# Inverting the recurrence's 32x32 blocks whole on VectorE, instead of joining 16x16 inverses by matmuls

## The chip, the cores and the metric

The kernel runs on one NeuronCore of a Trainium2 chip. The metric is the device time of one execution in microseconds (us). A core has five engines that each work through a queue of their own in order: TensorE (PE; its weight loads are shown as PEld), VectorE (DVE), ScalarE (ACT), GpSimd (POOL) and SyncE (SP), which here only starts DMAs. Results of matmuls go to PSUM, everything else lies in SBUF, and larger intermediates in device memory (HBM).

## What is computed

The reference is two transformer blocks on 1024 tokens of width 1024. The first block has gated linear attention, windowed attention and a feed-forward part. The second has an even layer (retention and an RWKV-7 recurrence, in both directions, over 1024 tokens and 256 tokens of context) and an odd layer (long convolutions and neighbourhood attention). The change concerns the RWKV-7 recurrence alone. Per head it is

```python
def rwkv7_scan(r, w, k, v, kk, a, s0):
    def step(s, inp):
        r_t, w_t, k_t, v_t, kk_t, a_t = inp
        sa = jnp.einsum('bhvk,bhk->bhv', s, -kk_t)
        s = s * w_t[:, :, None, :] + sa[..., None] * (kk_t * a_t)[:, :, None, :] + v_t[..., None] * k_t[:, :, None, :]
        return s, jnp.einsum('bhvk,bhk->bhv', s, r_t)
    ...
```

The kernel does it in chunks of 64 tokens. Within a chunk the terms `sa` of all tokens solve a triangular system: a unit lower triangular 64x64 matrix per head and chunk has to be inverted. Its two diagonal 32x32 blocks are inverted first, then joined by the off-diagonal block.

## The kernel before

All five engines' code is written as one Python program; a list scheduler of the framework decides, before the run, in which order each engine's instructions stand. It prefers what is written earlier in the program, as soon as it holds it to be ready, and fills the gaps with what is written later. That order is then fixed: an engine that waits for one instruction holds up all that stand behind it. In `mixers` the recurrence (`rwkv`) is written first and the retention projections (`ret_proj`) after it, so in the queue of TensorE projection matmuls (L217 to L219) fill the gaps of the recurrence. When they are used up, `ret_state` follows (matmuls L1370, and a chain on GpSimd), and the next stage begins when both it and the recurrence are done.

The recurrence has two directions of ten 128-token tiles. A batch is one tile of each direction, 64 blocks of 32x32 in all (2 directions, 2 chunks, 8 heads, 2 diagonal blocks). There are ten batches, and each goes through four parts:

- **Preparation** (`prep2`): decays, products and the four score matrices per chunk by matmuls (L1604, L1613, L1649, L1655); VectorE masks them out of PSUM (`wam`, L1657). The triangular blocks are written to HBM (`wlt`, L1661).
- **Inversion** (`invert`): L is loaded from HBM with one block half per partition, 128 partitions for 64 blocks of two diagonal 16x16 halves. VectorE then does a substitution column by column: a product with the known columns (`wtm`, L1681), then a reduction (L1682), 15 of each. The 16x16 inverses are written to HBM (`wrd`, L1684).
- **Merge** (`merge`, once per direction): the 16x16 inverses (`wdc`, L1696) and the 16x16 off-diagonal parts (`wnr`, L1697) are loaded; ScalarE spreads them into masked tiles (L1701, L1702), VectorE transposes (`wD`, L1703), and TensorE joins two 16x16 inverses to a 32x32 one with three groups of matmuls (L1709, L1712, L1721), with copies by ScalarE between and behind them (L1717, L1726). VectorE transposes the result (`wY`, L1731). Then the two 32x32 inverses are joined to the 64x64 one `wX` by two groups of matmuls (L1738, L1745) with ScalarE's copies (L1741, L1749).
- **Steps** (`chain`): two chunks per direction, four steps a batch. A step is five groups of matmuls (L1790, L1797, L1811, L1823, L1828). Between them stand copies by ScalarE and VectorE (`wrs`, L1793 and L1794; `wxv`, L1803 and L1805) and the state's update on VectorE (`wt`, L1816; `wxv`, L1782) and GpSimd (`wS`, L1783).

The order in the program is

```python
        prep(0)
        invert(0)
        prep(1)
        for bi in range(10):
            for s, (d, m) in enumerate(batches[bi]):
                merge(d, m, bi, s, bi)
            for s, (d, m) in enumerate(batches[bi]):
                chain(d, m, bi == 9)
            if bi < 9:
                invert(bi + 1)
            if bi < 8:
                prep(bi + 2)
```

so the inversion of the next batch has the steps of this one to hide behind, on the same VectorE. The tiles L, T and the products' tile have one buffer each. A step and a merge each take a two-bank PSUM tile (`p2`), of which there are two; a merge takes two in turn, one for the 16x16 joining and one for the rest.

Of the kernel before, what the change touches and what calls it, by code (L numbers as in the profile page):

```python
# [10 lines left out]
F32 = mybir.dt.float32  # L11
# [5 lines left out]
OP = mybir.AluOpType  # L17
AX = mybir.AxisListType
# [21 lines left out]
class Ker:  # L40
# [1507 lines left out]
    def rwkv(self, p):  # L1548
# [21 lines left out]
        T = p.tile([P, 16, 16], F32, name="wT")  # L1570

        hm = p.tile([P, 4], F32, name="whm")
        nc.sync.dma_start(hm, a["c_rwh"])

        N_ = p.tile([P, 8, 64], F32, name="wN")
        G_ = p.tile([P, 8, 64], F32, name="wG")
        for t in (N_, G_):
            nc.gpsimd.memset(t, 0.0)
# [4 lines left out]
        rt_d = [dr.tile([64, 2, 16, 16], F32, name=f"wrd{b}") for b in range(10)]  # L1583
# [3 lines left out]

        def by_rows(t, s, e, step, width, at):

            v = t[32 * s + 16 * e:32 * s + 16 * e + 16]  # L1590
            return bass.AP(tensor=v.tensor, offset=v.offset + at, ap=[[step, 64], [64 * step, 8], [1, width]])
# [76 lines left out]
        def invert(bi):  # L1668


            L = p.tile([P, 16, 16], F32, name="wL", tag="wL", bufs=1)
            for h in range(2):
                q = slice(16 * h, 16 * h + 16)
                nc.sync.dma_start(L[64 * h:64 * h + 64], lt_d[bi][:, q, q])
            nc.gpsimd.memset(T, 0.0)
            nc.gpsimd.memset(bass.AP(tensor=T.tensor, offset=T.offset, ap=[list(T.ap[0]), [17, 16]]), 1.0)
            tmp = p.tile([P, 256], F32, name="wtm", tag="wtm", bufs=1)
            for i in range(14, -1, -1):
                n = 15 - i
                tv = tmp[:, :n * n].rearrange("p (c j) -> p c j", j=n)  # L1680
                nc.vector.tensor_mul(tv, T[:, i + 1:, i + 1:], L[:, i:i + 1, i + 1:].to_broadcast([P, n, n]))  # L1681
                nc.vector.tensor_reduce(T[:, i + 1:, i], tv, axis=AX.X, op=OP.add, negate=True)  # L1682
            for h in range(2):
                nc.sync.dma_start(rt_d[bi][:, h], T[64 * h:64 * h + 64])  # L1684

        def merge(d, m, bi, s, xi):
# [3 lines left out]
            Y = p.tile([P, 2, 4, 32], F32, name="wY", tag="wY", bufs=1)  # L1690

            dc = p.tile([P, 8, 16], F32, name="wdc", tag="wdc", bufs=1)
            nr = p.tile([P, 8, 16], F32, name="wnr", tag="wnr", bufs=1)
# [990 lines left out]
```

## Time and profile before

| | us |
|---|---|
| median of 3 runs | 4260.48 (4253.2 to 4278.48) |
| profiled execution | 4259.86 |
| its span | 4258.1 |
| TensorE busy | 3871.4 (91%), 24649 instructions |
| TensorE weight loads busy | 3126.2 (73%) |
| VectorE busy | 1956.1 (46%), 2944 instructions |
| ScalarE busy | 1402.2 (33%), 2881 instructions |
| GpSimd busy | 1116.5 (26%), 1135 instructions |

Shares of the whole span are means over stages that have different limits. The recurrence runs from about 2123 to 2993 us. The views of the trace that are used below are: windows (busy time of each engine in a stretch, then the granted TensorE clock, the DMA share and GB/s), waits (who waited for whom, inferred from semaphores), groups of instructions by line, and the timeline (instructions in order of time, with what ended the idle time before them in brackets). In the windows the columns are PE, PEld, DVE, ACT and POOL where all engines are shown, and PE and PEld alone for a line of TensorE. In a group the columns are: line, engine, operation, output <- inputs, shapes, count, busy us, mean ns of one, and the idle time before them with its releasers. Where one row shows "+4 forms", its mean is over several shapes. Matmuls are pipelined and their ends are modelled, so a busy TensorE is not one at its peak.

### The profile page before, as it was taken

How to read it: one execution, taken by the hardware profiler on the slowest of the kernel's cores; microseconds unless marked ns; L12 is line 12 of the kernel's file. 1: busy time of each engine (PE TensorE's matmuls, PEld its weight loads, DVE VectorE, ACT ScalarE, POOL GpSimd, SP SyncE). 2: the span in 40 equal slices, each digit the busy share in tenths (PEclk: the TensorE clock that was granted, in tenths of full speed). 3: DMA queues.
4: the chain of work that ended last, by engine and by line, in shares of the span. 5: the costliest groups of instructions: out<-in, count | busy, mean ns of one | idle time of the engine just before them, and what ended most of it. 6: DMA issues, size and time to landing. Idle time of an engine off the chain costs nothing. (4 is left out here: it accounts for less than half of the span.)

```text
span 4258.1 us, 62069 instructions
## 1 busy us (share of the span) xinstructions
PE 3871.4 (91%) x24649; PEld 3126.2 (73%) x24649; DVE 1956.1 (46%) x2944; ACT 1402.2 (33%) x2881; POOL 1116.5 (26%) x1135
## 2 busy tenths in 40 slices
PE   7999989988999999699879898988789999998987
PEld 5788867776878888577777787777467777676776
DVE  4233433456443443633234444442556426653576
ACT  4333332215212222532244353443223324442211
POOL 1110202123111111201364233226530200003574
PEclk9999979998999999788898899986899999998998
DMA  5322237562141413332576555553764644324465
GB/s 200 122 97 77 89 105 257 207 242 102 57 151 60 139 63 101 138 140 102 184 218 172 165 139 147 165 151 106 229 200 144 235 134 119 104 77 152 153 199 202
DMA packets 474209, 621.96 MB, mean 146 GB/s; under 512 B 163201, under 2 KB 324403, under 8 KB 467776
## 3 DMA queue, kind: packets, MB, share of 16 engines
q1 hardware_dynamic: 423440, 416.26, 30.2%
q0 software_dynamic: 50480, 201.75, 14.4%
q8 instruction: 194, 3.18, 0.3%
q14 instruction: 95, 0.78, 0.1%
HBM read 423.34 MB, written 193.88 MB: 145 GB/s over the span
## 5 line engine op out<-in xcount | busy, mean ns | idle before, releaser
L217 PE MATMUL p<-hhi,whi 128*128 128x512 f32 x1056 | 417.1, 396 | 5.9 <-DVE hf L389 5.8
L218 PE MATMUL p<-hlo,whi 128*128 128x512 f32 x1056 | 415.7, 394 | 4.3 <-DVE hlo L391 4.3
L219 PE MATMUL p<-hhi,wlo 128*128 128x512 f32 x1056 | 415.0, 393 | 0.0
L217 PE MATMUL pf<-whi,hhi 128*128 128x512 f32 (+1 forms) x992 | 358.8, 363 | 19.1 <-ACT rqr L1279 10.3
L218 PE MATMUL pf<-wlo,hhi 128*128 128x512 f32 (+1 forms) x992 | 353.8, 357 | 7.7 <-POOL wlo L177 4.3
L219 PE MATMUL pf<-whi,hlo 128*128 128x512 f32 (+1 forms) x992 | 352.1, 356 | 0.0
L176 ACT CAST whi<-wraw 128x2048 fp32r<-128x2048 f32 (+1 forms) x123 | 193.1, 1574 | 457.1 <-PE pt L219 174.8
L177 DVE TENSOR_TENSOR wlo<-wraw,whi 128x2048 fp32r<-128x2048 f32 (+1 forms) x103 | 213.4, 2073 | 271.5 <-ACT whi L176 265.5
L217 PE MATMUL pf<-hhi,whi 128*128 128x512 f32 (+1 forms) x640 | 254.1, 397 | 4.4 <-ACT hyo L2047 1.5
L219 PE MATMUL pf<-hhi,wlo 128*128 128x512 f32 (+1 forms) x640 | 250.2, 391 | 2.5 <-DMA wlo<-wkl 2.5
L218 PE MATMUL pf<-hlo,whi 128*128 128x512 f32 (+1 forms) x640 | 250.0, 391 | 0.0
L217 PEld LDWEIGHTS pf<-whi,hhi 128*128 128x128 f32 x992 | 199.7, 202 | 58.7 <-ACT rqr L1279 11.2
L217 PE MATMUL pj<-whi,hhi 128*128 128x512 f32 (+1 forms) x560 | 216.7, 389 | 27.3 <-ACT whi L176 12.1
L217 PEld LDWEIGHTS p<-hhi,whi 128*128 128x128 f32 x1056 | 201.3, 191 | 54.3 <-DVE hf L389 6.2
L218 PEld LDWEIGHTS p<-hlo,whi 128*128 128x128 f32 x1056 | 201.0, 190 | 46.7 <-DVE hlo L391 5.3
L219 PEld LDWEIGHTS p<-hhi,wlo 128*128 128x128 f32 x1056 | 200.9, 190 | 43.1 <-issue 0.8
L218 PEld LDWEIGHTS pf<-wlo,hhi 128*128 128x128 f32 x992 | 200.0, 202 | 35.3 <-issue 6.6
L219 PE MATMUL pj<-whi,hlo 128*128 128x512 f32 (+1 forms) x560 | 214.2, 384 | 3.5 <-DVE hlo L381 3.5
L219 PEld LDWEIGHTS pf<-whi,hlo 128*128 128x128 f32 x992 | 198.9, 201 | 23.7 <-issue 2.6
L218 PE MATMUL pj<-wlo,hhi 128*128 128x512 f32 (+1 forms) x560 | 214.7, 384 | 0.3 <-DVE wlo L177 0.3
L217 PEld LDWEIGHTS pf<-hhi,whi 128*128 128x128 f32 x640 | 123.2, 193 | 36.1 <-issue 7.4
L217 PEld LDWEIGHTS pj<-whi,hhi 128*128 128x128 f32 x560 | 108.4, 194 | 54.6 <-ACT whi L176 12.3
(762 smaller groups left out, 8591.2 us busy)
## 6 DMA issues: line engine op xcount, KB each, us to landing
wraw<-w_in POOLq DMA_DIRECT2D x25, 1024.0 KB, 6.0
wraw<-w_ada POOLq DMA_DIRECT2D x24, 1024.0 KB, 7.8
wraw<-w_up POOLq DMA_DIRECT2D x22, 1024.0 KB, 6.1
whi<-wkh POOLq DMA_DIRECT2D x40, 512.0 KB, 5.4
wlo<-wkl POOLq DMA_DIRECT2D x40, 512.0 KB, 5.4
wraw<-ada_w POOLq DMA_DIRECT2D x32, 512.0 KB, 4.7
ox<-x SPq DMA_DIRECT2D x48, 256.0 KB
xp<-xl SPq DMA_DIRECT2D x48, 256.0 KB
```

What stands on the lines that cost most here:

```text
L176: nc.scalar.copy(hi[:, :n], raw[:, :n])
L177: self.we.tensor_sub(lo[:, :n], raw[:, :n], hi[:, :n].bitcast(F32))
L217: mm(out, L[0], R[0], start=first, stop=False)
L218: mm(out, L[0], R[1], start=False, stop=False)
L219: mm(out, L[1], R[0], start=False, stop=last)
```

## The change

The 32x32 blocks are inverted whole. L is loaded with all 32 rows of a block on a partition, as one contiguous 4 KB piece; each block stands on two partitions, and the one takes the even rows of the inverse, the other the odd rows (16 each). GpSimd writes -1 on L's diagonal and 1 on the inverse's, so that one formula holds for all rows. The substitution has 31 columns, each a product and a reduction. The inverse is written to HBM in rows of 128 bytes (`rt_d`), and a merge loads it with a row per partition (`wV`): that is the operand that `wY` was, and four transposes on VectorE per merge make the diagonal blocks of `wX` from it. All of the 16x16 joining goes: the loads of `wdc` and `wnr`, the masked tiles, the transpose `wD`, three groups of matmuls, and ScalarE's copies. A merge needs one `p2` tile instead of two. Line numbers shift: L1681 and L1682 become L1670 and L1671, `wX`'s transposes are L1687, L1738 and L1745 become L1694 and L1701, and the steps' matmuls L1746, L1753, L1767, L1779 and L1784.

```diff
-        T = p.tile([P, 16, 16], F32, name="wT")
+        T = p.tile([P, 16, 32], F32, name="wT")
...
-        rt_d = [dr.tile([64, 2, 16, 16], F32, name=f"wrd{b}") for b in range(10)]
+        rt_d = [dr.tile([64, 32, 32], F32, name=f"wrd{b}") for b in range(10)]
...
         def invert(bi):
-            L = p.tile([P, 16, 16], F32, name="wL", tag="wL", bufs=1)
+            L = p.tile([P, 32, 32], F32, name="wL", tag="wL", bufs=1)
             for h in range(2):
-                q = slice(16 * h, 16 * h + 16)
-                nc.sync.dma_start(L[64 * h:64 * h + 64], lt_d[bi][:, q, q])
+                nc.sync.dma_start(L[64 * h:64 * h + 64], lt_d[bi])
+            nc.gpsimd.memset(bass.AP(tensor=L.tensor, offset=L.offset, ap=[list(L.ap[0]), [33, 32]]), -1.0)
             nc.gpsimd.memset(T, 0.0)
-            nc.gpsimd.memset(bass.AP(tensor=T.tensor, offset=T.offset, ap=[list(T.ap[0]), [17, 16]]), 1.0)
-            tmp = p.tile([P, 256], F32, name="wtm", tag="wtm", bufs=1)
-            for i in range(14, -1, -1):
-                n = 15 - i
-                tv = tmp[:, :n * n].rearrange("p (c j) -> p c j", j=n)
-                nc.vector.tensor_mul(tv, T[:, i + 1:, i + 1:], L[:, i:i + 1, i + 1:].to_broadcast([P, n, n]))
-                nc.vector.tensor_reduce(T[:, i + 1:, i], tv, axis=AX.X, op=OP.add, negate=True)
             for h in range(2):
-                nc.sync.dma_start(rt_d[bi][:, h], T[64 * h:64 * h + 64])
+                th = T[64 * h:64 * h + 64]
+                nc.gpsimd.memset(bass.AP(tensor=th.tensor, offset=th.offset + h, ap=[list(th.ap[0]), [34, 16]]), 1.0)
+            tmp = p.tile([P, 16 * 32], F32, name="wtm", tag="wtm", bufs=1)
+            for i in range(30, -1, -1):
+                r0, n = (i + 1) // 2, 32 - i
+                tv = tmp[:, :(16 - r0) * n].rearrange("p (r j) -> p r j", j=n)
+                nc.vector.tensor_mul(tv, T[:, r0:, i:], L[:, i:i + 1, i:].to_broadcast([P, 16 - r0, n]))
+                nc.vector.tensor_reduce(T[:, r0:, i], tv, axis=AX.X, op=OP.add, negate=True)
+            rv = rt_d[bi].rearrange("k (r h) i -> h k r i", h=2)
+            for h in range(2):
+                nc.sync.dma_start(rv[h], T[64 * h:64 * h + 64])
...
         def merge(d, m, bi, s, xi):
...
+            V = p.tile([P, 2, 4, 32], F32, name="wV", tag="wV", bufs=2)
...
             for e in range(2):
-                nc.vector.transpose(Y[r1[e]].rearrange("p c i k -> p (c i) k"),
-                                    X[r1[e], :, :, 0:32].rearrange("p c i k -> p (c i) k"))
+                for b in range(2):
+                    rw = (r1, r2)[b][e]
+                    nc.sync.dma_start(V[rw].rearrange("p c i k -> p (c i) k"), units(rt_d[bi], s)[:, e, b])
+                    nc.vector.transpose(X[rw, :, :, 32 * b:32 * b + 32].rearrange("p c i k -> p (c i) k"),
+                                        V[rw].rearrange("p c i k -> p (c i) k"))
...
-                    nc.tensor.matmul(pp[e][r2[e], 32 * n:32 * n + 32], of[n // 4][r1[e], n % 4], Y[r1[e], n // 4, n % 4],
+                    nc.tensor.matmul(pp[e][r2[e], 32 * n:32 * n + 32], of[n // 4][r1[e], n % 4], V[r1[e], n // 4, n % 4],
```

The scheduler makes new orders from this. The first place is the queue of TensorE where the projection matmuls (`pf`) end. Before, it reads as follows; the numbered `p` tiles are the steps' PSUM tiles, four per batch, and 20092, 20154 and 20216 are the second to fourth step of batch 8 (batches count from 0 to 9):

```order
L218 MATMUL pf<-hlo,whi 128x256
L219 MATMUL pf<-hhi,wlo 128x256
L1823 MATMUL p_20092<-wS,wrr 64x64 x8
L1828 MATMUL p_20092<-wxv,wam 64x64 x8
L1811 MATMUL p_20154<-wxv,wbt 64x64 x8
L1823 MATMUL p_20154<-wS,wrr 64x64 x8
L1828 MATMUL p_20154<-wxv,wam 64x64 x8
L1790 MATMUL p_20216<-wxv,wam 64x64 x8
L1709 MATMUL p_20321<-wdT,wN 64x32 x16
L1712 MATMUL p_20321<-wD,ident 64x256 x2
L1797 MATMUL p_20216<-wrs,wX_0_13940 64x64 x8
L1370 MATMUL pf<-rvl,rkd 128x64 x8
```

Behind the last projection row stand 10 of the 20 step groups of batch 8, and the merges and steps of batch 9. In the changed kernel the last projection row is followed by the end of batch 7 (19004 is its fourth step), and 19337 is the first merge of batch 8:

```order
L219 MATMUL pf<-hhi,wlo 128x256
L1636 MATMUL pj<-ident,wbk 128x128 x4
L1642 MATMUL pj<-wkr,wbk 128x128 x4
L1767 MATMUL p_19004<-wxv,wbt 64x64 x8
L1642 MATMUL pj<-wkr,wbk 128x128 x4
L1636 MATMUL pj<-ident,wbk 128x128 x4
L1779 MATMUL p_19004<-wS,wrr 64x64 x8
L1784 MATMUL p_19004<-wxv,wam 64x64 x8
L1642 MATMUL pj<-wkr,wbk 128x128 x8
L1370 MATMUL pf<-rvl,rkd 128x64 x2
L1694 MATMUL p_19337<-wV,wof 32x32
```

So the same projections now end one batch earlier in the recurrence's order. Ahead of the first merge stand 390 projection and 121 preparation matmuls (415 and 100 before).

The second place is the queue of VectorE inside the steps of batch 7, from the copy `wrs` of its second step on. Before:

```order
L1794 COPY wrs<-p_19414 64x256
L1703 STREAM_TRANSPOSE wD<-wdT 128x256
L1805 TENSOR_SCALAR wxv<-p_19414 64x4x64
L1794 COPY wrs<-p_19476 64x256
L1816 TENSOR_TENSOR wt_19444<-p_19414,wS 64x256 x2
L1782 TENSOR_TENSOR wxv<-wt_19444,wfc 64x4x64 x2
L1805 TENSOR_SCALAR wxv<-p_19476 64x4x64
L1657 TENSOR_TENSOR wam<-pj,wmk 128x512 x2
L1816 TENSOR_TENSOR wt_19506<-p_19476,wS 64x256 x2
```

Now:

```order
L1750 COPY wrs<-p_18880 64x256
L1670 TENSOR_TENSOR wtm<-wT,wL 128x128
L1671 TENSOR_REDUCE wT<-wtm 128x8
L1670 TENSOR_TENSOR wtm<-wT,wL 128x136
L1671 TENSOR_REDUCE wT<-wtm 128x8
L1670 TENSOR_TENSOR wtm<-wT,wL 128x162
L1671 TENSOR_REDUCE wT<-wtm 128x9
L1670 TENSOR_TENSOR wtm<-wT,wL 128x171
L1671 TENSOR_REDUCE wT<-wtm 128x9
L1761 TENSOR_SCALAR wxv<-p_18880 64x4x64
L1670 TENSOR_TENSOR wtm<-wT,wL 128x200
L1750 COPY wrs<-p_18942 64x256
```

Between the two copies of one step there stood one transpose; now eight instructions of the inversion stand there. Before, the inversion was over by the first step of its batch; now it runs through all four steps.

## Rows read from the trace of the kernel before

**Rows 1.** Whole core, filled stretch and tail: length, busy us (instructions) by engine

```profile
2225.00:2905.00 680.00, 603.59 (x7518) 515.35 (x7518) 315.84 (x689) 302.88 (x803) 224.34 (x359) 0.90 0.54 157
2905.00:2993.00 88.00, 70.14 (x850) 64.25 (x845) 18.93 (x40) 35.10 (x91) 74.59 (x79) 0.62 0.28 81
```

**Rows 2.** The same view, TensorE lines L1709, L1712, L1721 alone, in this order

```profile
2225.00:2905.00 680.00, 24.85 (x576) 21.50 (x576) 0.90 0.54 157
2225.00:2905.00 680.00, 12.70 (x72) 4.58 (x72) 0.90 0.54 157
2225.00:2905.00 680.00, 24.21 (x576) 21.02 (x576) 0.90 0.54 157
```

**Rows 3.** The same view, TensorE lines L1790 and L1828 alone, in this order

```profile
2225.00:2905.00 680.00, 30.68 (x560) 24.30 (x560) 0.90 0.54 157
2225.00:2905.00 680.00, 25.23 (x542) 20.43 (x544) 0.90 0.54 157
```

**Rows 4.** Waits of TensorE in the filled stretch: us in total, times, longest us

```profile
PE p L1738 <- DVE wT L1682: 9.1, 2, 8.4
PE p L1811 <- DVE wxv L1805: 8.9, 6, 4.1
PE p L1797 <- DVE wrs L1794: 7.0, 3, 4.7
PE pj L1649 <- DVE wbk L1633: 6.0, 3, 2.5
PE p L1721 <- ACT wG L1717: 6.1, 6, 1.7
```

**Rows 5.** Groups of VectorE instructions in the filled stretch, columns as on the page

```profile
L1681 DVE TENSOR_TENSOR wtm<-wT,wL 128x1 f32<-128x1 f32 (+4 forms) x135 | 45.0, 333 | 57.8 <-DMA wL<-wlt 53.7
L1782 DVE TENSOR_TENSOR wxv<-wt,wfc 64x256 f32<-64x256 f32 x68 | 39.8, 585 | 2.1
L1682 DVE TENSOR_REDUCE wT<-wtm 128x1 f32<-128x1 f32 (+4 forms) x135 | 32.2, 238 | 4.3
L1731 DVE STREAM_TRANSPOSE wY<-wX 32x256 f32<-32x256 f32 x36 | 15.5, 431 | 21.8 <-ACT wX L1726 21.5
```

**Rows 6.** The same view by shape, 2120 to 3000 us, reductions of L1682

```profile
L1682 DVE TENSOR_REDUCE wT<-wtm 128x15 f32<-128x225 f32 x10 | 3.9, 389 | 0.3
L1682 DVE TENSOR_REDUCE wT<-wtm 128x1 f32<-128x1 f32 x10 | 1.5, 148 | 0.3
```

**Rows 7.** Timeline of TensorE: start us, us; first merge, last merge and steps

```profile
2236.28 0.24 PE L1738 MATMUL p<-wY,wof 32*32 32x32 f32 x2
...
2928.34 1.14 PE L1738 MATMUL p<-wY,wof 32*32 32x32 f32 x32 [5.20 <-ACT wX L1726]
...
2934.01 1.06 PE L1745 MATMUL p<-wX,wQ 32*32 32x32 f32 x32
...
2949.72 1.12 PE L1790 MATMUL p<-wxv,wam 128*64 128x64 f32 x16
...
2988.35 1.12 PE L1828 MATMUL p<-wxv,wam 128*64 128x64 f32 x16
```

**Rows 8.** Groups of VectorE instructions in the tail

```profile
L1782 DVE TENSOR_TENSOR wxv<-wt,wfc 64x256 f32<-64x256 f32 x8 | 6.7, 842 | 0.2
```

**Rows 9.** Timeline of VectorE: end of the first inversion and first transpose

```profile
2217.10 0.38 DVE L1682 TENSOR_REDUCE wT<-wtm 128x15 f32<-128x225 f32 x1
...
2224.25 0.45 DVE L1703 STREAM_TRANSPOSE wD<-wdT 128x256 f32<-128x256 f32 x1 [6.18 <-ACT wdT L1701]
```

**Rows 10.** Waits of VectorE in the filled stretch

```profile
DVE wtm L1681 <- DMA wL<-wlt: 53.7, 8, 13.4
DVE wrs L1794 <- ACT wrs L1793: 49.5, 15, 8.4
DVE wam L1657 <- PE pj L1655: 47.2, 25, 3.7
DVE wxv L1805 <- ACT wxv L1803: 44.2, 16, 5.5
```

More of the change, by code (lines that the diff above doesn't have):

```diff
@@ L1699, in merge @@
-            D_ = p.tile([P, 8, 32], F32, name="wD", tag="wD", bufs=1)
-            for h in range(2):
-                nc.scalar.mul(dT[:, :, 16 * h:16 * h + 16], dc, hm[:, h:h + 1])
-                nc.scalar.mul(N_[:, :, 32 * h + 16:32 * h + 32], nr, hm[:, 2 + h:3 + h])
-            nc.vector.transpose(D_, dT)
-            v = self.p2()
-            vv = [v[:, 0:512], v[:, 512:1024]]
-            RW = [slice(0, 64), slice(64, 128)]
-            for n in range(8):
-                for e in range(2):
-                    nc.tensor.matmul(vv[e][RW[e], 32 * n:32 * n + 32], N_[RW[e], n], dT[RW[e], n],
-                                     start=True, stop=True, tile_position=(64 * e, 64 * e))
@@ L1711, in merge @@
-            for e in range(2):
-                nc.tensor.matmul(vv[e][RW[e], 256:512], self.ident[RW[e], RW[e]], D_[RW[e]].rearrange("p n k -> p (n k)"),
-                                 start=True, stop=False, tile_position=(64 * e, 64 * e))
-            for e in range(2):
-                for b in range(2):
-                    r0 = 64 * e + 32 * b
-                    nc.scalar.mul(G_[r0:r0 + 32, :, 32 * b:32 * b + 32],
-                                  vv[e][r0:r0 + 32, 0:256].rearrange("p (n k) -> p n k", k=32), -1.0)
@@ L1719, in merge @@
-            for n in range(8):
-                for e in range(2):
-                    nc.tensor.matmul(vv[e][RW[e], 256 + 32 * n:288 + 32 * n], G_[RW[e], n], D_[RW[e], n],
-                                     start=False, stop=n == 7, tile_position=(64 * e, 64 * e))
-            for e in range(2):
-                for b in range(2):
-                    r0 = 64 * e + 32 * b
-                    nc.scalar.copy(X[r0:r0 + 32, :, :, 32 * b:32 * b + 32].rearrange("p c i k -> p (c i) k"),
-                                   vv[e][r0:r0 + 32, 256:512].rearrange("p (n k) -> p n k", k=32))
+            V = p.tile([P, 2, 4, 32], F32, name="wV", tag="wV", bufs=2)
@@ L2595, in constants @@
     c["c_rwm"] = m
-    pq = (np.arange(P) // 16) % 4
-    c["c_rwh"] = np.stack([pq % 2 == 0, pq % 2 == 1, pq == 0, pq == 2], 1).astype(np.float32)
     nm = np.full((4, 32, 2, 23, 40), NEG, np.float32)
```

17 lines of the change are left out of this document (removed).

## The prediction, made before the changed kernel was run

> **What bounds the kernel now.** I read the windows first, then the waits, then the timeline. In the windows [rows 1] the recurrence has two parts. In the filled stretch, 2225 to 2905 us, TensorE is busy 603.6 of 680 us (89%), and VectorE 315.8 (46%). In the tail, 2905 to 2993 us, the projection matmuls have run out: TensorE's granted clock is 0.62 and VectorE works 18.9 of 88 us. The reader should see that the two parts have different limits. In the first TensorE has 76.4 us idle in all, so work taken from it is worth nearly its own length; in the second the dependent steps of the recurrence set the end. The waits [rows 4] say who makes TensorE idle: the four largest rows that name VectorE add up to 31.0 us. VectorE itself mostly waits for others [rows 10], so before the change it has slack. The timeline [rows 7] gives the pace: nine batches from 2236.28 to 2928.34 us, 76.9 us each.
>
> The sum is made against the profiled execution, 4259.86 us (span 4258.1), which is 0.6 us under the median of the runs, 4260.48.
>
> **Removed from TensorE.** The joining matmuls are busy 24.85 + 12.70 + 24.21 = 61.8 us in the filled stretch [rows 2], 18 of the 20 merges. TensorE waited 6.1 us more inside them for ScalarE's copy [rows 4]. Both go: **-67.9 us**. By the Trainium skill, "Perfetto Trace Analysis", section Identifying the Most-Contended Engine, matmul busy time is a poor measure because matmuls are pipelined, and weight-load busy time is the one to use. By weight loads the same three lines hold 21.50 + 4.58 + 21.02 = 47.1 us [rows 2], and the total below would end 14.7 us higher, at about 4243. I take the matmul figure, since the rows alternate with fill whose own overlap is counted the same way.
>
> **Moved.** The order of TensorE's queue shows that the last projection matmul now stands ahead of the merges of batch 8; before, it stood in the middle of the steps of batch 8. The two merges of that batch and the 10 step groups that stood ahead of it pass from the filled stretch to the tail. A group costs 30.68/35 = 0.88 us (L1790) to 25.23/34 = 0.74 us (L1828) [rows 3], so 10 are 8.1 us; two merges are 2 x (1.14 + 1.06) = 4.4 us [rows 7]. The filled stretch loses **-12.5 us**, and the tail gets them back below. Without VectorE the stretch would last 680 - 80.4 = 600 us.
>
> **Added to VectorE.** An inversion had 30 instructions over 1240 products per partition; it has 62 over 5592. Reductions cost 148 ns for one product and 389 for 225 [rows 6]: 1.076 ns per product and 147 ns each. So 31 new ones take 31 x 0.147 + 5592 x 0.001076 = 10.6 us. A multiplication costs 333 - 238 = 95 ns more than its reduction on the average [rows 5], so 31 take 13.5 us. One inversion is 24.1 us against (45.0 + 32.2)/9 = 8.6 us. Eight transposes per batch of 0.431 us [rows 5] replace four of that shape and two over all 128 partitions. VectorE's work in the stretch: 315.8 - 77.2 (old inversions) - 15.5 - 7.8 (old transposes; the 18 wider ones at the 0.431 of the nearest row) + 8 x 24.1 + 64 x 0.431 = 436 us, 73% of 600 where it was 46%.
>
> What TensorE loses by this no row shows, since VectorE was never so full. If its waits for VectorE grow as the work, 31.0 x 436/316, they cost 12 us more. If they grow as busy over idle time, from 0.46/0.54 to 0.73/0.27, they are 3.1 times as long, 65 us more. I take **+32 us**, a little under the middle: the order puts the new instructions between the recurrence's own, into gaps where VectorE waited 49.5, 47.2 and 44.2 us [rows 10], so part of the work fills time that was idle.
>
> **The start.** The first inversion is 15.5 us longer, and the first merge waits for it. TensorE has 390 projection and 121 preparation matmuls queued ahead of that merge (415 and 100 before), so most of it is covered: **+5 us**, between 0 and 15.5.
>
> **The tail.** It now holds batches 8 and 9 instead of half of 8 and all of 9. A batch's steps took 2988.35 + 1.12 - 2949.72 = 39.75 us [rows 7]. From the first L1738 to the first step it was 21.4 us, with a joining in between; one merge alone took 2934.01 + 1.06 - 2928.34 = 6.7 us. I take 10 us for two merges in a row. Twice 10 + 39.75 is 99.5 us against 88: **+11.5 us**. If the last merges overlap the steps of batch 8, as the order allows, it is 0; with 21.4 us for each pair it is 34. The last inversion also stands in this stretch. In the tail VectorE's two-input products took 842 ns against 585 before it [rows 5, 8]; 31 x 0.257 = 8.0 us more makes that inversion 32 us. With 6.8 us from the end of an inversion to the next transpose (2217.48 to 2224.25) [rows 9] and 3.4 us of transposes that is 42 us, under the 49.75 of a batch, so it does not decide.
>
> **At nothing.** ScalarE loses 240 copies; it was busy 302.9 of 680 us [rows 1], and only the 6.1 us counted above waited for it. SP issues four loads per merge as before, but all four now wait for the inversion, where two of the four only read data long stored; the 6.8 us above covers that, and if not, it lengthens every batch (second rival). GpSimd clears a diagonal of L after L's load; it is busy 224 of 680 us [rows 1], so the instruction is free, but the wait behind that load (53.7 us in all for VectorE, 13.4 at the longest [rows 10]) now stands in GpSimd's queue ahead of the weight loads and of wS. I give it no price of its own; it is in the upper end of VectorE's.
>
> **Sum.** -67.9 - 12.5 + 32 + 5 + 11.5 = -31.9: **4228 us**, 0.75% faster. All low ends: -80.4 + 12 + 0 + 0 = -68, 4191. All high ends: -80.4 + 65 + 15.5 + 34 = +34, 4294.
>
> **Rivals.** *The time is given back in waits.* If the extra waits are 65 us, the upper end above, the sum is +1: 4261 us, no change. For it: 73% in one queue that serves the recurrence in order, and an order that was fixed before the run. Against it: VectorE's large waits now are for others.
>
> *VectorE's loop becomes the pace.* An inversion must follow the batch's preparation, and the next merge must follow the inversion, so a batch cannot be shorter than that loop. VectorE's work is 436/8 = 54.5 us per batch. Add the wait for L, 53.7/8 = 6.7, the way back through memory, 6.8, and the waits for preparation, steps and copies that stay in the queue, (47.2 + 49.5 + 44.2)/9 = 15.7 [rows 9, 10]: 83.7 us if none of them is covered. The place is the last product of an inversion, with the stored rows, the four loads and the transposes behind it. With eight loops the stretch is 11 + 8 x the loop; with +16.5 for start and tail the kernel is slower once the loop passes (680 - 16.5 - 11)/8 = 81.6 us. At 83.7 us it is 4277; with the longest wait for L, 13.4, in every batch the loop is 90.4 and the time 4330. I put this case at 4300, a loop of 86.6 us. Against it: the new products can run while the steps wait.
>
> *The change does not do what it says* is not open: the new order has none of the joining matmuls.
>
> **Chances.** A measurement of this kernel can tell about 0.5% (21 us) from no change. Forecast, faster by more than that: 0.43. Given back: 0.30. VectorE's loop: 0.27. The forecast's own range is 4191 to 4238. Cases of both signs hold most of the chance, so the range that should hold 8 in 10 goes from 4190 over the second case into the third, to 4320.
>
> **What would show it.** Right: the projections run out near 2862 us (2225 + 600 + 32 + 5), TensorE is busy some 83% and VectorE some 69% of the stretch before that, the waits for VectorE come to 50 to 80 us, and the tail is about 100 us. An inversion of 24 us would confirm the price. Wrong by the first rival: the projections run out near 2895 us and the waits for VectorE are near 100 us. Wrong by the second: batches 82 us or more apart, TensorE's merge matmuls waiting for the transposes, and VectorE waiting little. A tail of 120 us or more would make the tail the failed step.

## The result and the profile after

The changed kernel takes 4200.34 us (median of 4 runs, 4195.8 to 4209.2), against 4260.69 us before on the same chip. The ratio is 0.9855 with a 95% interval from 0.9819 to 0.9892: 60 us less, 46 to 77 by the interval. The direction was forecast and the time lies in the range, but the gain is about twice the 32 us of the forecast. The profiled execution takes 4202.26 us, its span is 4199.8.

First the windows. The columns are as in [rows 1]. Of the kernel before, the whole of the recurrence, from 2123 us to the first matmul of the next stage (L405):

```profile
2123.00:2993.00 870.00, 755.05 (x8933) 653.79 (x8932) 367.59 (x783) 375.79 (x980) 366.46 (x536) 0.87 0.54 157
```

Of the kernel after, the same stage, then its filled stretch (to the last projection matmul) and its tail:

```profile
2123.00:2931.00 808.00, 686.09 (x7530) 596.38 (x7528) 545.74 (x1122) 292.69 (x738) 375.61 (x539) 0.86 0.58 174
2225.00:2807.00 582.00, 516.68 (x5888) 443.31 (x5887) 413.16 (x889) 215.55 (x550) 233.09 (x374) 0.92 0.62 186
2807.00:2931.00 124.00, 90.12 (x1112) 81.68 (x1112) 77.21 (x144) 39.70 (x102) 83.88 (x93) 0.59 0.32 84
```

The stage is 62 us shorter. TensorE's busy time fell by 69.0 us, and its idle time (length less busy) rose from 115.0 to 121.9 us. Behind the stage nothing was gained: from 2993 us to the end of the span it was 1265 us, from 2931 it is 1269. The two parts of [rows 1] moved against each other: the filled stretch went from 680 to 582 us, where 637 were forecast, and the tail from 88 to 124, where 99.5 were.

What TensorE waited for in the filled stretch (us in total, times, longest us), which answers to [rows 4]:

```profile
PE p L1694 <- DMA wV<-wrd: 23.5, 7, 9.1
PE pf L217 <- DMA whi<-wkh: 7.8, 4, 4.1
PE p L1753 <- DVE wrs L1750: 6.3, 4, 4.8
...
PE pj L1591 <- DVE wam L1644: 3.0, 2, 2.0
PE pf L217 <- DVE zt L1311: 2.1, 2, 1.6
PE pj L1636 <- DVE wbk L1620: 1.9, 3, 0.7
...
PE pf L217 <- DVE wtm L1670: 0.7, 1, 0.7
```

The five rows here that name VectorE add up to 14.0 us, with five smaller ones to 16.3. Before, the four of [rows 4] had 31.0 and these four 9.3 more, 40.3 in all:

```profile
PE p L1738 <- DVE wtm L1681: 4.2, 1, 4.2
PE p L1738 <- DVE wY L1731: 2.3, 3, 1.0
PE p L1823 <- DVE wt L1816: 1.5, 3, 1.0
PE pf L217 <- DVE zt L1311: 1.3, 1, 1.3
```

The largest wait is new: merges wait 23.5 us in all for the loads of V. These loads stand behind the inversion, so this too is in part a wait for VectorE, through memory; with all of it the sum is 39.8 us, no more than before. VectorE's groups in the same stretch answer to [rows 5]:

```profile
L1670 DVE TENSOR_TENSOR wtm<-wT,wL 128x512 f32<-128x512 f32 (+30 forms) x247 | 103.0, 417 | 17.8 <-POOL wL L1661 10.2
L1671 DVE TENSOR_REDUCE wT<-wtm 128x15 f32<-128x465 f32 (+30 forms) x247 | 84.2, 341 | 7.7
...
L1687 DVE STREAM_TRANSPOSE wX<-wV 32x256 f32<-32x256 f32 x64 | 27.9, 436 | 43.5 <-DMA wV<-wrd 41.9
```

An inversion is 31 x (0.417 + 0.341) = 23.5 us, priced at 24.1, and a transpose 0.436, priced at 0.431. VectorE is busy 413.2 of 582 us, 71%. So the prices and the load were right, and yet TensorE's waits for VectorE did not grow. TensorE's timeline says where the recurrence stands (first merge, last projection matmul, first merge of the last batch, last step, next stage):

```profile
2236.70 0.31 PE L1694 MATMUL p<-wV,wof 32*32 32x32 f32 x2 [2.97 <-DMA wV<-wrd]
...
2806.40 0.28 PE L219 MATMUL pf<-hhi,wlo 128*128 128x256 f32 x1
...
2900.22 1.01 PE L1694 MATMUL p<-wV,wof 32*32 32x32 f32 x29
...
2926.11 1.12 PE L1784 MATMUL p<-wxv,wam 128*64 128x64 f32 x16
2931.04 0.24 PE L405 MATMUL pf<-ident,colr 8*128 8x8 f32 x1 [3.81 <-DMA colr<-rw_ln_b]
```

Nine batches take 663.5 us, 73.7 each, where it was 76.9 [rows 7]. But the projections are out 97 us earlier than in the kernel before, while the last step is only 62 us earlier. Their last matmul before:

```profile
2903.57 0.28 PE L219 MATMUL pf<-hhi,wlo 128*128 128x256 f32 x1
```

The recurrence now trails the projections by 120 us; before, by 86. That became the starting point of the experiments: two strands share TensorE's queue, the recurrence and the projections with `ret_state` behind them, and the stage ends with the later one.

### The profile page after: what moved, and what is told of

It is laid out like the page before. It is cut to its first block, busy times and chain, and to the rows that moved or that the text cites. A ratio compares the mean times of both kernels' runs of the same rounds, so it can differ in the third digit from the quotient of the medians.

```text
span 4199.8 us, 59342 instructions
## 1 busy us (share of the span) xinstructions
PE 3812.9 (91%) x23289; PEld 3077.8 (73%) x23289; DVE 2130.2 (51%) x3284; ACT 1320.4 (31%) x2641; POOL 1129.9 (27%) x1153
## 5 line engine op out<-in xcount | busy, mean ns | idle before, releaser
L219 PE MATMUL p<-hhi,wlo 128*128 128x512 f32 x1056 | 413.8, 392 | 0.0
L219 PE MATMUL pf<-whi,hlo 128*128 128x512 f32 (+1 forms) x992 | 349.3, 353 | 0.0
L219 PE MATMUL pf<-hhi,wlo 128*128 128x512 f32 (+1 forms) x640 | 249.4, 390 | 0.0
L217 PE MATMUL pj<-whi,hhi 128*128 128x512 f32 (+1 forms) x560 | 216.5, 389 | 26.5 <-ACT whi L176 12.1
L219 PEld LDWEIGHTS p<-hhi,wlo 128*128 128x128 f32 x1056 | 200.0, 189 | 42.6 <-issue 0.8
L219 PE MATMUL pj<-whi,hlo 128*128 128x512 f32 (+1 forms) x560 | 214.1, 383 | 3.0 <-DVE hlo L381 3.0
L219 PEld LDWEIGHTS pf<-whi,hlo 128*128 128x128 f32 x992 | 198.5, 200 | 22.1 <-issue 1.3
L1670 DVE TENSOR_TENSOR wtm<-wT,wL 128x2 f32<-128x2 f32 (+30 forms) x310 | 145.7, 470 | 37.5 <-POOL wL L1661 28.0
```

The costliest lines, as they stand in the source:

```text
L217: mm(out, L[0], R[0], start=first, stop=False)
L219: mm(out, L[1], R[0], start=False, stop=last)
L1670: nc.vector.tensor_mul(tv, T[:, r0:, i:], L[:, i:i + 1, i:].to_broadcast([P, 16 - r0, n]))
```

## The experiments

The scheduler decides the order of every queue anew for each kernel, so the last one asks how much an order alone can do. Medians and ratios to the kernel before are over all runs of each; "the stage" is 2123 us to the first L405 of the profiled execution. The chain of `ret_state` on GpSimd can run on beyond that matmul, and then part of its cost lies behind the stage.

**Most of VectorE's added load taken away, the joining still gone.** Only 15 of the 31 columns are computed.

```diff
-            for i in range(30, -1, -1):
+            for i in range(30, 15, -1):
```

> The changed kernel with 16 fewer of the 31 columns: only columns 30 to 16 are computed (15 products and 15 reductions, 680 products per partition instead of 5592), the other columns of the inverse stay those of the identity, so VectorE's work of an inversion falls from about 24 us to about 8 us, close to what it was before the change, and everything else of the changed kernel stays. Theory A (VectorE's added work lies in its idle time; the gain is the joining matmuls' busy time, all of it): the filled stretch stays within 10 us; only the last inversion, which stands in the tail with little beside it, gives up to 20 us: 4180 to 4200 us. Theory B (VectorE's added work does cost the 32 us of the prediction, and the shorter merge pays them back unseen): 4200 - 32 - 20, 4140 to 4165 us.

(The 15 products hold 716 elements, not the 680 of the text.) Measured: 4210.19 us, ratio 0.9874 (0.9858 to 0.9891): no faster than the full inversion, so neither theory's number. The profile shows why. By its window the stage is 22 us shorter, with TensorE's busy time the same, and the work behind it is 33 us longer (4210.7 - 2909 = 1302, against 1269):

```profile
2123.00:2909.00 786.00, 687.43 (x7558) 595.80 (x7557) 380.10 (x814) 295.84 (x744) 352.69 (x528) 0.88 0.63 186
```

The strands have changed places. In the view of single lines (x count, then shortest, median and longest ns, then first and last start us) the last step (L1784) and the last addition of the retention states on GpSimd (L1383, the end of `ret_state`) stand so, first with half the columns, then in the changed kernel:

```profile
L1784 PE MATMUL p<-wxv,wam x640: 222/222/367, 2243.1 to 2835.0; 128*64 128x64 f32 x160
L1383 POOL TENSOR_TENSOR rS<-rS,rtm x18: 1250/1259/1277, 2878.3 to 2958.0; 64x512 f32<-64x512 f32 x18
```

```profile
L1784 PE MATMUL p<-wxv,wam x640: 222/222/367, 2263.2 to 2926.9; 128*64 128x64 f32 x160
L1383 POOL TENSOR_TENSOR rS<-rS,rtm x18: 1254/1262/1521, 2837.9 to 2911.6; 64x512 f32<-64x512 f32 x18
```

With the short inversion the recurrence is done 92 us earlier, but it takes TensorE's time from the projections, whose last matmul starts at 2858.7 (`2858.73 0.28 PE L219 MATMUL pf<-hhi,wlo 128*128 128x256 f32 x1`) instead of 2806.4. `ret_state` then runs alone, into the next stage. With the full inversion the recurrence ends last, and the chain on GpSimd hides beside it. VectorE's added work costs TensorE 23 us of idle time in the stage (98.6 to 121.9). Almost none of it lies in the filled stretch: with half the columns, TensorE is idle there for 634.0 - 570.4 = 63.6 us, in the changed kernel for 65.3.

```profile
2225.00:2859.00 634.00, 570.43 (x6791) 487.97 (x6790) 334.36 (x736) 236.50 (x608) 245.97 (x392) 0.91 0.62 183
```

It lies in what follows the last projection matmul, 14.6 us idle with half the columns and 33.9 in the changed kernel. The kernel gets these 23 us back behind the stage, where the chain no longer runs alone.

**The joining matmuls put back as dead work.**

```diff
...
+            for g in range(3):
+                for n in range(8 if g != 1 else 1):
+                    for e in range(2):
+                        w = 32 if g != 1 else 256
+                        o = 32 * n + (256 if g == 2 else 0)
+                        nc.tensor.matmul(pp[e][RJ[e], o:o + w], jl[n // 4][RJ[e], n % 4], jr[n // 4][RJ[e], o:o + w],
+                                         start=True, stop=True, tile_position=(64 * e, 64 * e))
```

(`jl` and `jr` are the batch's `wrr` and `wbt`, `RJ` the two halves of the partitions.)

> The changed kernel with matmuls of the joining's shapes and counts put back into every merge as dead work (16 of 64x64 by 32 columns, 2 by 256, 16 by 32 columns; operands that lie ready long before, results overwritten). No copy, load or transpose comes back. Theory A: TensorE's idle time stays as it is and the time rises by the rows' busy length, 20 merges at 61.8/18 us, 62 to 75 us in all: 4262 to 4275 us, so about the time before the change. Theory C (the matmuls were half hidden in the idle time of TensorE, and the gain came from the merge's shorter chain of loads, copies and transposes): +15 to +40 us, 4215 to 4240 us.

Measured: 4342.31 us, ratio 1.0188 (1.017 to 1.0206): 142 us more than the changed kernel, twice what theory A said, and far above C. The windows of this kernel, the stage and 2500 to 2915 us, then the dead rows alone (L1700) in the stage:

```profile
2123.00:3045.00 922.00, 795.74 (x8902) 690.27 (x8904) 529.53 (x1135) 298.43 (x745) 346.42 (x524) 0.81 0.53 159
2500.00:2915.00 415.00, 369.28 (x4576) 316.68 (x4574) 277.19 (x614) 128.75 (x339) 117.25 (x209) 0.82 0.45 129
2123.00:3045.00 922.00, 76.32 (x1360) 65.52 (x1360) 0.81 0.53 159
```

And of the changed kernel:

```profile
2500.00:2801.00 301.00, 264.37 (x3018) 227.75 (x3018) 206.04 (x452) 104.03 (x273) 101.20 (x178) 0.91 0.63 188
```

The dead rows are busy 76.3 us, but TensorE's busy time in the stage rose by 109.7. At a mean granted clock of 0.82, where the changed kernel has 0.91, the other rows are longer too: the projection matmuls of L219 with 512 columns take 445 ns instead of 416, those of L1642 331 instead of 295. TensorE's idle time rose by only 4 us (126.3). The other 33 us lie behind the stage (1302 against 1269 us): here too the projections are the later strand, the last step being at 2954 and the last projection at 2998. So this work on TensorE costs its length and more, and it was not half hidden in idle time; C is out.

**The same dead work on sparse operands.** Against the kernel with the dead work above:

```diff
-                        nc.tensor.matmul(pp[e][RJ[e], o:o + w], jl[n // 4][RJ[e], n % 4], jr[n // 4][RJ[e], o:o + w],
+                        nc.tensor.matmul(pp[e][RJ[e], o:o + w], self.ident[RJ[e], RJ[e]], Xs[d][xi % NB][RJ[e]].rearrange("p c i k -> p (c i k)")[:, o:o + w],
```

> The kernel of dead_joining (+142 us) with the same dead matmuls on other operands: the identity as weights and the block diagonal X of the merge two batches earlier as moving data, both mostly zeros as the operands of the kernel before were (there masked tiles and the identity), where dead_joining read dense tiles. In dead_joining the granted clock of 2500 to 2915 us was 0.82, against 0.91 in the changed kernel and 0.90 in the kernel before. If the clock's fall belongs to dense operands, the clock comes back to 0.88 or more, the rows to 62 to 70 us, and the time is 4262 to 4300. If it belongs to having the extra matmuls without the copies and waits of the real joining between them, the clock stays near 0.82 and the time at 4320 to 4345.

The edit does not quite do this. X is the tile that this merge's own transposes have just written, not that of two batches earlier, so the dead matmuls now wait for the transposes (`PE p L1700 <- DVE wX L1687`: 8.3 us, nine times, from 2123 to 3027 us), which the dense ones did not. And X, with its triangular blocks, is only about half zeros. Measured: 4321.47 us, ratio 1.0135 (1.0106 to 1.0164). The clock came back in part, in the windows of the stage and of 2500 to 2890 us:

```profile
2123.00:3027.00 904.00, 776.13 (x8906) 673.42 (x8908) 532.92 (x1135) 299.40 (x745) 344.95 (x524) 0.84 0.54 162
2500.00:2890.00 390.00, 346.82 (x4394) 297.08 (x4393) 265.12 (x590) 129.54 (x337) 109.14 (x201) 0.87 0.48 137
```

The clock is between the two cases of the expectation; the time is that of the second, at its lower end. Of the 121 us over the changed kernel, 90 are busy time of the stage, 6 idle time, and 25 lie behind the stage (4321.2 - 3027 = 1294 us), where `ret_state` runs on.

**VectorE's load added to the kernel before.**

```diff
...
+                dv = tmp.rearrange("p (r j) -> p r j", j=16)
+                nc.vector.tensor_mul(dv, L, L[:, 0:1].to_broadcast([P, 16, 16]))
+                nc.vector.tensor_reduce(ds, dv, axis=AX.X, op=OP.add, negate=True)
                 nc.vector.tensor_mul(tv, T[:, i + 1:, i + 1:], L[:, i:i + 1, i + 1:].to_broadcast([P, n, n]))
```

> The kernel before, with VectorE's work of the new inversion and nothing else: each of the 15 columns gets a second product and reduction over 256 elements as dead work ahead of its own (5080 products per partition in 60 instructions instead of 1240 in 30; the new inversion has 5592 in 62). VectorE gets some 14 us more per inversion, on the path to the merge as in the change. Theory A: the work lies in idle time: 4260 to 4272 us. Theory B: the prediction's own term for these waits, +32 us, and a few us for the tail: 4285 to 4305 us. If it is over 4320 the kernel before had less slack on VectorE than the changed one.

Measured: 4289.73 us, ratio 1.0062 (1.0041 to 1.0083), 27 us slower (17 to 35): theory B's size, not A's. The windows of the stage, 26 us longer, of its filled stretch and of the rest:

```profile
2123.00:3019.00 896.00, 771.77 (x8906) 664.43 (x8906) 516.75 (x1082) 375.90 (x979) 370.00 (x530) 0.84 0.52 152
2225.00:2871.00 646.00, 576.09 (x6798) 489.41 (x6797) 399.84 (x865) 275.01 (x725) 218.22 (x344) 0.89 0.56 162
2871.00:3019.00 148.00, 114.80 (x1553) 101.52 (x1553) 76.31 (x149) 62.32 (x167) 86.26 (x96) 0.63 0.27 70
```

Of the 26 us 17 are busy time and 9 idle, at a clock of 0.84 instead of 0.87. (The profiled execution, 4297.63 us, is 8 us over the median; behind its stage it has 12 us more than the kernel before.) Here too the projections end earlier, at 2871.1 us instead of 2903.6, and what follows them in the stage is 148 us instead of 88; TensorE's idle time in the filled stretch is 69.9 us, where it was 76.4. Taken alone, VectorE's part of the change costs about what the prediction said, but not where it said.

**The products done twice.**

```diff
+                for _ in range(2):
-                nc.vector.tensor_mul(tv, T[:, r0:, i:], L[:, i:i + 1, i:].to_broadcast([P, 16 - r0, n]))
+                    nc.vector.tensor_mul(tv, T[:, r0:, i:], L[:, i:i + 1, i:].to_broadcast([P, 16 - r0, n]))
```

> The changed kernel with each of the 31 products of an inversion done twice (the same output): about 12 us more of VectorE per inversion, VectorE's share of the filled stretch from 71% to about 87%. Theory A with slack left: +0 to +15 us in the filled stretch and up to +20 us in the tail, 4200 to 4235 us. Theory B (waits grow as busy over idle time): 0.87/0.13 against 0.71/0.29 is 2.7 times the waits, +40 to +60 us and the tail, 4250 to 4280 us. If the loop from inversion to merge sets the pace already (73.6 us a batch), each of eight batches gets the whole 12 us: +96 us and the tail, 4300 us or more.

Measured: 4328.32 us, ratio 1.0156 (1.0134 to 1.0178): the last case, the loop. TensorE's timeline has the first merge of the first and of the last batch:

```profile
2260.63 0.31 PE L1695 MATMUL p<-wV,wof 32*32 32x32 f32 x2 [5.58 <-DMA wV<-wrd]
...
3026.88 0.28 PE L1695 MATMUL p<-wV,wof 32*32 32x32 f32 x2 [21.98 <-DMA wV<-wrd]
```

Nine batches take 766.3 us, 85.1 each: 11.4 more than the 73.7 of the changed kernel, for 31 products of 0.392 us, 12.2 us. With half the columns it is (2787.57 - 2210.17)/9 = 64.2. So 16 us more of inversion cost 9.5 us a batch up to the changed kernel, and 12 more cost 11.4: the changed kernel stands where VectorE's loop begins to set the pace. The projections end at 2805 us as in the changed kernel, the last step at 3053. Past this point the filled stretch is hit as well: TensorE is idle 580.0 - 490.9 = 89.2 us in it, not 65.3.

**The retention states' chain left out.** In the three kernels (half the columns, the changed one, the one before) the same three lines go:

```diff
-                tm = pl.tile([P, 8, 64], F32, name="rtm", tag="rtm", bufs=2)
-                nc.gpsimd.tensor_mul(tm[rows], S_[rows, t], gch[rows, :, None].to_broadcast([64, 8, 64]))
-                nc.gpsimd.tensor_add(S_[rows, n], S_[rows, n], tm[rows])
```

> The kernel of half_columns (15 of 31 columns; 4210 us, ratio 0.9874) without the retention states' carry on GpSimd: the 16 products and 16 additions (L1382, L1383) of ret_state are left out, 36 us of GpSimd. The theory now (D): two strands share TensorE, the recurrence's batches, and the projections with ret_state behind them; the stage ends with the later one. In half_columns the recurrence was done at 2835 us and the projections at 2859, and ret_state's chain on GpSimd ran on to 2959 with nothing of the recurrence beside it. So without it: 30 to 50 us less, 4160 to 4180. The rival (E): TensorE's busy time alone sets the stage, and the chain hides behind the next stage: less than 10 us, 4200 to 4210.

> The changed kernel without the same 32 GpSimd instructions (the retention states are not carried on). Theory D: the chain ended at 2913 us, 14 us before the recurrence's last step, so it does not set the end; what is left is that VectorE's products ran 735 ns in the tail beside GpSimd and 417 ns before it, 33 of them, up to 10 us: 4185 to 4200. If the two engines' disturbing each other decides the tail: 4175 or less. Theory E: 4195 to 4205.

> The kernel before without the same 32 GpSimd instructions. Before, the chain was the last to end (2993.1 us; the last step at 2989.5), GpSimd was busy 74.6 of the tail's 88 us, and the last batch needed 61 us from its merge to its last step, against 27 in the changed kernel. Theory D: both strands end within 4 us, so taking the chain away gives only what the steps gain by a free GpSimd and TensorE's ret_state matmuls in one piece: 10 to 25 us, 4236 to 4250. Theory E: 4255 to 4263.

(There are 18 of each, not 16, some 41 us of GpSimd.) Measured: half the columns 4167.84 us, ratio 0.9769 (0.9728 to 0.9811), 42 us less than with the chain; the changed kernel 4197.53 us, 0.9845 (0.981 to 0.988), 3 us less, within the uncertainty; the kernel before 4250.86 us, 0.997 (0.9954 to 0.9986), 13 us less. D's intervals hold the first two, and the third is 1 us over its upper end; E's miss the first by 32 us and the third by 4. With half the columns the stage kept its length (next stage at 2913 us instead of 2909), and the 42 us are all behind it (1302 to 1260 us): the chain had run on there. So two strands race, and the chain costs 42 us, nothing that can be told from noise, or 13 us as the recurrence covers it or not. The stages without the chain, of the kernel before, half the columns and the changed one:

```profile
2123.00:2979.00 856.00, 749.85 (x8918) 648.63 (x8916) 369.61 (x782) 376.04 (x979) 327.11 (x495) 0.87 0.55 160
2123.00:2913.00 790.00, 685.61 (x7563) 594.39 (x7561) 381.74 (x814) 295.83 (x744) 339.26 (x521) 0.88 0.62 186
2123.00:2923.00 800.00, 691.03 (x7558) 601.15 (x7557) 532.51 (x1122) 293.76 (x739) 339.83 (x513) 0.86 0.60 177
```

Without the chain, VectorE's added work costs 4197.5 - 4167.8 = 30 us by the medians (about 32, with the two ratios' intervals some 23 either way). The two profiled executions differ by 35 us, and only 10 of these are in the stage (next stage at 2913 and 2923 us); the other 25 are behind it, and their cause stays open (13 of them are busy time of TensorE, at a mean granted clock of 0.93 against 0.95).

**Less for VectorE, less for GpSimd to wait for.** First the two copies of a step that VectorE makes go to ScalarE:

```diff
-                nc.vector.tensor_copy(rs[RW[1]], u[RW[1], 0:256])
+                nc.scalar.copy(rs[RW[1]], u[RW[1], 0:256])
...
-                        nc.vector.tensor_scalar(xv[RW[e], :, e], src, -1.0, None, op0=OP.mult)
+                        nc.scalar.mul(xv[RW[e], :, e], src, -1.0)
```

> The changed kernel with the two copies of a step that VectorE makes (L1750 wrs and L1761 wxv, 0.42 us each, 80 in all) moved to ScalarE, which then makes both halves one after the other. VectorE loses about 3.4 us a batch and the steps no longer stand behind an inversion's products with these two copies; a step gets some 0.8 us longer by ScalarE's second halves. If VectorE's cost (half_no_states against after_no_states: 30 us) comes from steps that queue behind products on VectorE: 10 to 25 us less than the changed kernel's 4200, 4175 to 4190. If it comes from the inversion's own length ahead of the merge: the steps' 0.8 us more, twice or four times a batch, eat the little that VectorE gains: 4198 to 4220.

Measured: 4206.6 us, ratio 0.9865 (0.984 to 0.989), the same as the changed kernel and the second case's number, though not for its reason. The batches did get shorter, (2880.28 - 2240.49)/9 = 71.1 us, but the last projection moved from 2806 to 2830 us and the last step stayed at 2926: again what one strand gains the other pays. Then GpSimd's queue:

```diff
-        T = p.tile([P, 16, 32], F32, name="wT")
...
-            nc.gpsimd.memset(bass.AP(tensor=L.tensor, offset=L.offset, ap=[list(L.ap[0]), [33, 32]]), -1.0)
-            nc.gpsimd.memset(T, 0.0)
+            nc.vector.memset(bass.AP(tensor=L.tensor, offset=L.offset, ap=[list(L.ap[0]), [33, 32]]), -1.0)
+            T = p.tile([P, 16, 32], F32, name="wT", tag="wT", bufs=2); nc.gpsimd.memset(T, 0.0)
```

> The changed kernel with two buffers for T (GpSimd's clearing of T no longer waits for the store of the inverse before) and with the diagonal of L written by VectorE instead of GpSimd (no wait for L's load in GpSimd's queue). In the filled stretch GpSimd waited 25.7 us for the one and 22.1 us for the other, with the weight loads and wS behind it. If these waits cost what TensorE waited behind them (7.8 + 5.8 us for weights and hidden states that GpSimd and SP load): 5 to 14 us less, 4186 to 4195. If GpSimd's queue has room for them, as the prediction had it: 4195 to 4205.

> Both edits together (copies_on_act and gpsimd_free). If the two costs are separate, the sum of what each gives, down to 4165; if both only shift waits within the recurrence while the projections and ret_state are the later strand, no more than the better of the two alone, and up to 4220 where the chain of ret_state comes to stand alone at the end, as it did in half_columns.

Measured: 4233.91 us, ratio 0.9926 (0.9905 to 0.9948), for GpSimd's queue alone, some 30 us slower than the changed kernel where 5 to 14 less or none was expected; with both edits 4205.39 us, 0.9871 (0.9844 to 0.9898), no different from the copies alone. The slower one has its last projection at 2848 us, 42 later than the changed kernel, its last step at 2944, 17 later, and 20 us more behind the stage. Why it came out so is not settled. None of these versions beats the changed kernel.

**An order alone.**

```diff
-            for s, (d, m) in enumerate(batches[bi]):
+            for s, (d, m) in reversed(list(enumerate(batches[bi]))):
                 merge(d, m, bi, s, bi)
```

> The changed kernel with the two merges of a batch written in the other sequence (direction 1 first): no instruction more or less, but a different order in every queue, since the list scheduler decides it anew. It says how much of the differences between these runs an order alone can make. If orders matter little: 4192 to 4210 us, and gpsimd_free's 33 us more are its own doing. If an order alone moves the time by 20 us or more either way, 4180 or less or 4220 or more, then gpsimd_free is no evidence on GpSimd's queue, and VectorE's 30 us and the 27 us of before_full_dve are sizes with that uncertainty.

Measured: 4203.07 us, ratio 0.9892 (0.9867 to 0.9917) (the kernel before beside it: 4255.52 us). By the medians that is 3 us from the changed kernel; by the two ratios it is 16, with some 19 either way from their intervals. The stage's window is 811 us long where it was 808:

```profile
2123.00:2934.00 811.00, 697.98 (x7542) 605.33 (x7540) 541.24 (x1122) 293.70 (x739) 377.59 (x543) 0.85 0.59 174
```

But the same instructions are busy 12 us more and TensorE is idle 9 us less than in the changed kernel. And the projections end at 2820 us where it was 2806. So this order moved the total by no amount that can be told from noise, but the division into busy and idle, and into filled stretch and tail, holds only to some 10 to 15 us. One order sets no bound for others: the 30 us of GpSimd's queue alone may still be one.

## Why the prediction was right, and where its sizes were off

That the time lies in the range is in part luck. The range, 4190 to 4320, holds gains and losses alike, and the time is 10 us above its lower end. Of the signs given for the forecast, the price of an inversion (23.5 us) and VectorE's load (71%) came true. The projections ended at 2806 us instead of 2862, TensorE was busy 89% of the filled stretch instead of 83%, and the tail took 124 us instead of 100. A tail of 120 us or more was named as the sign that the tail is the failed step. In the sum a filled stretch 55 us shorter than forecast (582 against 637) and a tail 24.5 us longer offset each other in part.

**Joining removed (-67.9).** The mechanism held, and TensorE's busy time does set most of the stage. From the kernel before to half the columns, where VectorE's inversions are about as short as before (15 x (0.320 + 0.203) = 7.8 us against 8.6), busy time falls by 67.6 us and idle time by 16.4, 84 us in the stage. But there the chain on GpSimd runs on behind the stage. In the same pair without the chain, busy time falls by 64.2 us and idle time by 1.8, 66 us in all; by the medians of that pair it is 83 us, some 19 either way. So the size was about right, perhaps low. (The prediction's 61.8 us are of 18 of the 20 merges.) By weight loads the term would have been 14.7 us smaller, and the measured total went the other way: as the price of removed work, matmul busy time was the nearer measure here. The Trainium skill, "Perfetto Trace Analysis", section Identifying the Most-Contended Engine, gives weight-load busy time for judging how close TensorE is to its roofline, which is another question. No run takes the joining out of the kernel before by itself, so each pair differs by the loads' shapes and by the orders of the queues too.

**VectorE (+32, start +5).** The step that failed is "what TensorE loses by this", told as waits of TensorE in the filled stretch. Those waits were to be 50 to 80 us; they are 16.3 by the rows that name VectorE and 39.8 with the loads behind the inversion, no more than before. TensorE's queue has projections to do in the meantime; a slower inversion hardly makes it wait but lets the projections go ahead, and the bill comes when they are used up. So the filled stretch got 98 us shorter instead of 43, and the tail 36 us longer instead of 11.5. The size of the whole was near: 22 us in the stage from half the columns to all, 27 us (17 to 35) on the kernel before, and some 30 by the medians without the chain, where the prediction had 32 and 5. The start cost 0.4 us against the kernel before (2236.28 to 2236.70). That is not because the first inversion is covered: with half the columns the first merge comes at 2210.2, 26.5 us earlier. Its products began at 2181.2 us in the changed kernel and at 2202.8 before, an order that the prediction had not read. (One ratio of the prediction is a little off: 0.73/0.27 over 0.46/0.54 is 3.2, so its upper end for these waits would be 67 us, not 65.)

**The tail (+11.5).** Its step "batches 8 and 9 instead of half of 8 and all of 9" was right, its price of 99.5 us was not: 124 us. Two terms were too small. Ahead of the first step of batch 8 the tail has 35.9 us (2807 to 2842.9), with the end of batch 7, the last preparation and the merges of batch 8, where 10 were priced. And the steps of batch 8 took longer: the last inversion, forecast at 32 us, took 38.7 (2839.3 to 2878.0) with these steps between its products. From the first matmul of the steps to the last it was 63 us (2842.9 to 2906.2), where a batch was priced at 39.75. Of these, TensorE waits 13.5 us for VectorE in the steps, and 25.5 us are `ret_state`'s matmuls (L1370). Two terms were too large. The merges of batch 9 ran beside the last steps of batch 8, and the steps of batch 9, with no inversion beside them, took 20 us (2907.0 to 2927.2). The price of 39.75 was no price of steps alone: in the stretch that it was read from, L1370 of the kernel before is busy 16.7 us, and in the last 20 us of the changed kernel it does not occur.

```profile
2949.72:2989.47 39.75, 16.68 (x72) 15.73 (x72) 0.54 0.16 44
```

**Left out.** The prediction's sum treats the stage as one queue. It has no term for the chain of `ret_state` on GpSimd, which costs 13 us before (6 to 20 by the ratio's interval) and not measurably after. The difference, some 10 us, may be a further part of the gain, but its uncertainty is larger than that.

Put together in the stage: -84 by the joining and +22 by VectorE are -62, where the prediction had -32, with +4 us behind the stage; the chain's share is inside these numbers. By the medians without the chain it is -83 and +30, with some -10 for the chain. The 28 us by which the forecast fell short are thus spread over terms that are each known to some 20 us, and how much belongs to which stays open.

**The rivals.** "Given back in waits" did not happen: the projections were out at 2806, not 2895. "VectorE's loop becomes the pace" named the right place, TensorE's merges waiting for what comes behind the inversion (23.5 us), but the price of 83.7 us a batch was 10 too high, since the batches came at 73.7. With 12 us more, at 85.1, past the 81.6 at which the prediction let it decide, it did decide: slower than before by 66 us.

## What to carry to other kernels

Where one engine's queue mixes a dependent strand with independent filling work, a slower producer in the strand can show up as an earlier end of the filling and a longer tail instead of as waits, until its loop sets the pace (the products done twice): follow each strand to its own end and ask which is later. Work removed from the shared engine was worth about its length here; time saved off it is worth only what the later strand gains, and can be nothing (half the columns, copies on ScalarE). Look for what runs behind the filling (here a chain on GpSimd) before deciding which strand should finish last.

## What the runs showed of the hardware that I had not expected

VectorE's two-input products in the tail are slower beside a busy GpSimd, and its reductions are not. VectorE's groups from 2807 to 2931 us, first of the changed kernel, then of the same without the retention chain (GpSimd busy 83.9 of 124 us in the one, 42.7 of 116 in the other):

```profile
L1670 DVE TENSOR_TENSOR wtm<-wT,wL 128x450 f32<-128x450 f32 (+30 forms) x34 | 25.6, 753 | 8.2 <-POOL wL L1661 7.2
L1671 DVE TENSOR_REDUCE wT<-wtm 128x15 f32<-128x450 f32 (+30 forms) x34 | 12.6, 369 | 1.1
L1738 DVE TENSOR_TENSOR wxv<-wt,wfc 64x256 f32<-64x256 f32 x14 | 11.5, 819 | 0.4
...
L1772 DVE TENSOR_TENSOR wt<-p,wS 64x256 f32<-64x256 f32 x14 | 5.9, 422 | 8.0 <-PE p L1767 7.7
```

```profile
L1670 DVE TENSOR_TENSOR wtm<-wT,wL 128x450 f32<-128x450 f32 (+30 forms) x34 | 18.1, 533 | 8.2 <-POOL wL L1661 7.1
L1671 DVE TENSOR_REDUCE wT<-wtm 128x15 f32<-128x450 f32 (+30 forms) x34 | 12.5, 369 | 1.1
L1738 DVE TENSOR_TENSOR wxv<-wt,wfc 64x256 f32<-64x256 f32 x14 | 9.0, 643 | 0.4
...
L1772 DVE TENSOR_TENSOR wt<-p,wS 64x256 f32<-64x256 f32 x14 | 5.9, 421 | 7.5 <-PE p L1767 7.3
```

Products with both inputs in SBUF go from 753 to 533 ns and from 819 to 643; the reductions stay at 369, and the sum with one input in PSUM (L1772) at 422. The Trainium skill, "SBUF — State Buffer", section Who interferes with whom, says that a VectorE instruction with two SBUF inputs contends with a GpSimd instruction that reads SBUF, and that a reduction does not; these rows agree.

The granted clock was lower with the dead matmuls on dense operands (0.82 from 2500 to 2915 us) than with as many on the identity and a tile about half zeros (0.87 from 2500 to 2890). The two kernels' queues are ordered differently too, and the second kernel's dead matmuls wait for transposes, so that the operands are the cause is suggested, not shown.
